# Requesting the first tiles of p_v from expert tile 118 on instead of 112, in a two-layer decoder trunk

## The chip, the cores and the metric

The kernel runs on one core of one Trainium2 chip. The metric is the device time of one execution in microseconds (us); the time of a kernel is the median of its runs. The profile is one execution, recorded by the hardware profiler; its times count from the start of its span.

## The reference

The program is a decoder trunk of two layers over 256 positions of width 1024. Each layer is an attention mixer (latent attention in layer 0, native sparse attention in layer 1) followed by a PEER feed-forward block, with a LayerNorm after each. Only the PEER block matters here. It holds 128 x 128 = 16,384 experts. Each position picks 16 experts for each of 8 heads by product keys, and the result is a sum over the picked experts:

```python
def peer_ffn(x, w_q, subkeys, u, v):
    ...
        experts = jnp.take_along_axis(cand_idx, pos, axis=-1)
        g = jax.nn.softmax(best, axis=-1)
        u_e = u[experts]
        v_e = v[experts]
        a = jax.nn.gelu(jnp.einsum("thkd,td->thk", u_e, xc, ...), approximate=False)
        return jnp.einsum("thk,thkd->td", (g * a).astype(v.dtype), v_e)
```

`u` and `v` are 16,384 x 1024 float32 each, 64 MB per layer and matrix.

## The kernel before

**Tiles.** All weights pass through one list, the stream, in the order in which they are used. For a PEER block the stream holds 128 tiles of `p_u` and then 128 tiles of `p_v`. A tile has 128 partitions x 1024 float32, which is 512 KB. The kernel does not gather experts for most positions: it multiplies every expert tile with 160 of the 256 positions (`xF`), and a matrix `A` holds the gate of each expert and position, zero where the expert was not picked. For the other 96 positions (partly for `u`, partly for `v`) it gathers single expert rows with indirect DMAs: 96 rows of 128 partitions x 4 KB from `p_ur`, then 64 from `p_v`.

**The u loop** (line 918) has one step per tile of `p_u`. `u_step(j)` runs 8 matmuls against `xF` (16 records in the profile, since each float32 matmul leaves two), straight from the tile that the DMA wrote. After every second step ScalarE applies gelu (`u_act`, L882) and VectorE multiplies it into `A` (L891). Between the steps VectorE also makes the one-hot matrices (`hot`, L759 to L770) that give the gates, and multiplies the gathered rows (`row`, L578).

**The v loop** uses the tiles of `p_v` in order. ScalarE rounds each to `hi` (L179), VectorE makes the remainder `lo` (L193), and TensorE multiplies both with parts of `A` (`W`, L900 and L905) into `acc`. In it VectorE adds the gathered rows of `p_v` (L600, L602).

**Who requests what.** All tiles are requested on SyncE's DMA queue (SP), which issues in the order of the program and waits, request by request, for the buffer to be free. Tiles of `p_u` are requested by `_snat` (line 149). From tile 96 on only five buffers serve them: tile j+5 is requested when TensorE has finished step j. Tiles of `p_v` are requested by `_sdma` (lines 120 and 125), two at a time as one request of 1024 KB where their place in the ring allows it. The pairs are (0,1), (2,3), (4,5), (6,7) in layer 0; in layer 1 tile 0 goes alone and then (1,2), (3,4), (5,6). They go to two rings of four tiles, `raw` and `spare`. The rows are requested by GpSimd (line 565) on a queue of its own, and a ring of six rows limits them.

**How far ahead of use p_v is requested.** `_ahead()` gives the last stream index that may be requested, and `self.vlim` caps it. At the start of a PEER block `vlim` is `v0 - 1`, where `v0` is the index of the first tile of `p_v`, so nothing of it is requested. At step `LATE` = 112 `gather()` sets up the second ring, `spare`. From that step on every even step raises `vlim` by 2:

```python
                u_step(j)
                if j == LATE:
                    self.gather()
                if j >= LATE and j % 2 == 0:
                    self.vlim += 2
```

`u_step` ends with `end()`, which first requests the next tile of `p_u`, then requests up to the limit that the step before had computed (`held`), and then computes a new one. A raise after step j is therefore seen at the end of step j+1 and put to use at the end of step j+2: the first tiles of `p_v` stand in SP's program behind the request that waits for step 114. After the loop `vlim` is lifted altogether. Independently of the limit, `nxt` of steps 125, 126 and 127 puts the `hi` copies of tiles 0, 1 and 2 of `p_v` into ScalarE's program, and those of 126 and 127 the `lo` of tiles 0 and 1 into VectorE's.

Of the kernel before, what the change touches and what calls it, by code (L numbers as in the profile page):

```python
# [42 lines left out]
SPREAD, LATE = 96, 112  # L43
# [4 lines left out]
class Kern:  # L48
# [471 lines left out]
    def peer(self, l):  # L520
# [3 lines left out]
        with ExitStack() as es:  # L524
# [44 lines left out]
            def g_x():  # L569
                for q in range(P // GX):  # L570
                    nc.gpsimd.dma_start(xrow[q * GX:q * GX + GX], self.hD[P - GT - GX:P - GT, 1, :])
                for hh in range(2):
                    nc.gpsimd.dma_start(gacc[hh * GT:hh * GT + GT], self.hD[P - GT:P, 1, :])

            def g_dot(k):
                a, c = order[k]
                t, x, d = grow.pop((a, c)), *((gacc, gdot) if a == "n" else (xrow, xdot))
                nc.vector.scalar_tensor_tensor(t, t, 1.0, x, op0=OP.mult, op1=OP.mult, accum_out=d[:, c:c + 1])  # L578
                if (a, c) == ("x", GX - 1):
                    g_row()  # L580
                    nc.scalar.activation(xdot, xdot, AF.Gelu)
                    self.defer(2, x_weights)
                g_row()
# [9 lines left out]
            def g_weights():  # L593
                nc.scalar.activation(gdot, gdot, AF.Gelu)
                nc.vector.tensor_tensor(ggate, ggate, gdot, op=OP.mult)
# [152 lines left out]
            def g_gen(hot):  # L748

                b4 = [P, 2, P, 2]  # L750
                for t0 in range(0, ND, 4):
                    while len(gq) == 2:
                        yield None
                    h = hot[:, t0 // 4 % 2]
                    if t0 >= NU:
                        h = h.bitcast(BF16)
                    oi, oj = h[:, 0], h[:, 1]
                    tt = nc.vector.tensor_tensor
                    tt(h[:, 0:2].rearrange("p w g i s -> p (w g) i s"), self.iota4[:, 0, None].to_broadcast([P, 4, P, 2]),  # L759
                       selI[:, t0 // 4].rearrange("p w (g s) -> p (w g) s", s=2)[:, :, None, :].to_broadcast([P, 4, P, 2]),  # L760
                       op=OP.is_equal); yield 0.64
                    if t0 < NU:
                        b5 = [P, 2, 2, P, 2]
                        tt(h[:, 2:4], oj[:, None].to_broadcast(b5),
                           selG[:, t0 // 4].rearrange("p w (g s) -> p w g s", s=2)[:, :, :, None, :].to_broadcast(b5), op=OP.mult)
                        gq.append((t0, oi, (h[:, 2], h[:, 3])))
                    else:
                        for o, i in ((h[:, 2], 0), (h[:, 3], 1), (oj, 2)):
                            x = selX[:, i, t0 - NU:t0 - NU + 4].rearrange("p (g s) -> p g s", s=2)
                            tt(o, oj, x[:, :, None, :].to_broadcast(b4), op=OP.mult)  # L770
                        gq.append((t0, oi, (h[:, 2], h[:, 3], oj)))
                    yield 0.64
# [4 lines left out]
            def g_flush(n=1):  # L777
                if len(gq) < n:
                    return
                while gq:  # L780
                    t0, oi, gs = gq.popleft()
                    ps = self.acc(t0 // 4 % 2)
                    for q in range(4):
                        for w, g in enumerate(gs):
                            self.mm(ps[:, q * P:(q + 1) * P], oi[:, q // 2, :, q % 2], g[:, q // 2, :, q % 2],
                                    w == 0, w == len(gs) - 1)
                    pv = ps.rearrange("p (t j) -> p j t", t=4)
                    k, sc_ = (done["a"], 1.0 / GS) if t0 < NU else (0, 1.0)
                    for x, j0, n in A:
                        m = min(max(k, 0), n)  # L790
                        if m > 0:
                            y = x[:, 0:m, t0:t0 + 4]
                            nc.vector.scalar_tensor_tensor(y, pv[:, j0:j0 + m], 1.0 / GS, y, op0=OP.mult, op1=OP.mult)  # L793
                        if m < n:
                            nc.scalar.activation(x[:, m:n, t0:t0 + 4], pv[:, j0 + m:j0 + n], AF.Copy, scale=sc_)  # L795
                        k -= n
                    done["g"] = t0 + 4
# [3 lines left out]
            def run_side(budget):  # L801
                credit[0] = min(credit[0] + budget, 2 * budget)
                paused = False
                while credit[0] > 0 and (first and not paused or second):
                    side = first if first and not paused else second
                    try:
                        cost = next(side[0])
                        if cost is None:
                            if paused or side is second:
                                return  # L810
                            paused = True
                        else:
                            credit[0] -= cost
                    except StopIteration:
                        side.popleft()
# [51 lines left out]
            def u_step(j):  # L867
                w, _ = self.nxt()
                if j % 2 == 0:
                    bank[j] = self.ps().rearrange("p (a t) -> p a t", a=2)  # L870
                ps = bank[j - j % 2][:, j % 2, 0:NU]
                for k in range(KC):
                    self.mm(ps, w[:, k * P:(k + 1) * P], xf[0][:, k, :], k == 0, k == KC - 1)
                self.end()
# [3 lines left out]
            def u_act(j):  # L878
                ps, n = bank.pop(j), min(done["g"], NU)
                y = slots((P - FIRST + j) % P, 2)  # L880
                if n:
                    nc.scalar.activation(ps[:, :, 0:n], ps[:, :, 0:n], AF.Gelu)  # L882
                    due.append((y[:, :, 0:n], ps[:, :, 0:n]))
                if n < NU:
                    nc.scalar.activation(y[:, :, n:NU], ps[:, :, n:NU], AF.Gelu)  # L885
                done["a"] = j + 2

            def u_mul():
                while due:
                    y, ps = due.pop()  # L890
                    nc.vector.tensor_tensor(y, y, ps, op=OP.mult)  # L891
# [16 lines left out]
            def w_start():  # L908
                W.append(self.pr8.tile([P, 5, 3 * P], F32R, tag="r8", name="W"))
                for j in range(3):  # L910
                    w_hi(j)
                w_lo(0)
                w_lo(1)
# [4 lines left out]
            for j in range(P):  # L918
                if j == 5:
                    g_x()  # L920
                g_flush(2)
                u_step(j)
                if j == LATE:
                    self.gather()
                if j >= LATE and j % 2 == 0:
                    self.vlim += 2
                self.slow = j < P - 7
                if j % 2:
                    u_mul()
                elif j:  # L930
                    u_act(j - 2)
                run_side(GB if len(A) > 1 else 2.1 if dj is None or j < dj else 1.15)
                if dj is None and gnext[0]:
                    dj = j + 2
                if not (first or second) and len(A) == 1:
                    es_r.close()

                    hot = self.pr8.tile([P, 2, 4, 2, P, 2], F16, tag="r8", name="hot")
                    A.append((pool(es_1, "slots1").tile([P, P - FIRST, ND], F32, name="A1"), 0, P - FIRST))
                    second.append(g_gen(hot))  # L940
                while dj and dc < len(order) and j >= dj + int((P - 6 - dj) / len(order) * dc):
                    g_dot(dc)
                    dc += 1
                    if dc == len(order):
                        g_weights()
                if done["g"] == ND and j >= P - 5 and not W:
                    w_start()
# [860 lines left out]
```

## Time and profile before

| | us |
|---|---|
| median of 3 runs | 1617.3 |
| lowest and highest run | 1615.9 and 1619.71 |
| the profiled execution | 1614.72 |
| its span in the profile | 1612.9 |

The profile lists, for each engine, its busy time and its instructions. PE is TensorE, DVE VectorE, ACT ScalarE, POOL GpSimd and SP SyncE. A row of the timeline gives start, duration, engine, line, operation and operands (written<-read), and in brackets how long the engine had been idle before and what it had waited for. PEclk is the share of its full clock that TensorE was granted. A row of the DMA view gives operands, queue, count, size and the median time from request to landing. The PEER block's u loop ends at 485.4 us in layer 0 and at 1311.9 us in layer 1.

### The profile page before, as it was taken

How to read it: one execution, taken by the hardware profiler on the slowest of the kernel's cores; microseconds unless marked ns; L12 is line 12 of the kernel's file. 1: busy time of each engine (PE TensorE's matmuls, PEld its weight loads, DVE VectorE, ACT ScalarE, POOL GpSimd, SP SyncE). 2: the span in 40 equal slices, each digit the busy share in tenths (PEclk: the TensorE clock that was granted, in tenths of full speed). 3: DMA queues.
4: the chain of work that ended last, by engine and by line, in shares of the span. 5: the costliest groups of instructions: out<-in, count | busy, mean ns of one | idle time of the engine just before them, and what ended most of it. 6: DMA issues, size and time to landing. Idle time of an engine off the chain costs nothing.

```text
span 1612.9 us, 27544 instructions
## 1 busy us (share of the span) xinstructions
PE 1559.4 (97%) x10018; PEld 1399.2 (87%) x10018; DVE 1396.6 (87%) x3245; ACT 683.1 (42%) x1355; POOL 517.6 (32%) x442
## 2 busy tenths in 40 slices
PE   7999999999989999999997999999999989999997
PEld 6779999999988888888885789999999978888886
DVE  5778798999949999999768789799999859999998
ACT  6555201222125555556466754111121245555553
POOL 2010134433325444331432210344343324443420
PEclk9999999999999999999999999999999999999999
DMA  7527999999998999998573258999999979999992
GB/s 241 196 89 232 351 409 408 409 408 345 394 375 319 368 371 343 356 355 296 188 259 96 67 183 282 400 408 409 408 398 354 385 307 390 355 361 343 364 352 92
DMA packets 140519, 510.76 MB, mean 317 GB/s; under 512 B 14144, under 2 KB 17248, under 8 KB 139296
## 3 DMA queue, kind: packets, MB, share of 16 engines
q1 hardware_dynamic: 90416, 325.75, 54.6%
q0 software_dynamic: 49968, 183.26, 30.0%
q8 instruction: 79, 1.29, 0.3%
q14 instruction: 56, 0.46, 0.1%
HBM read 503.19 MB, written 5.24 MB: 315 GB/s over the span
## 4 chain that ended last, share of the span: by engine, by line
PE 77%; DVE 11%; DMA 8%; ACT 2%; issue 1%; POOL 0%; SPq 0%; ACTq 0%; DVEq 0%; POOLq 0%
PE acc L273 44%; PE mm L273 31%; DMA row<-p_ur,xidx 5%; DVE row L578 3%; DMA nat<-p_u 3%; PE mm L300 1%; DVE hot L759 1%; DVE hot L770 1%; DMA xT<-xT 0%; DMA bounce<-ropeO 0%; DVE idx L641 0%; DVE lo L193 0%; DVE bnst L347 0%; ACT hi L179 0%; ACT p L1689 0%
## 5 line engine op out<-in xcount | busy, mean ns | idle before, releaser
L273 PE MATMUL acc<-hi,W 128*128 128x512 f32 x1452 | 409.1, 390 | 0.0
L273 PE MATMUL mm<-xF,nat 128*128 128x160 f32 x2304 | 328.7, 303 | 10.6 <-DMA nat<-p_u 10.5
L565 POOL DMA_INDIRECT row<-p_v,gidx x128 | 228.2, 1783 | 336.7 <-DVE gacc L602 257.7
L273 PEld LDWEIGHTS mm<-xF,nat 128*128 128x128 f32 x2304 | 320.0, 193 | 12.1 <-issue 11.4
L273 PEld LDWEIGHTS acc<-hi,W 128*128 128x128 f32 x1452 | 272.5, 188 | 57.5
L273 PE MATMUL acc<-lo,W 128*128 128x512 f32 x968 | 298.8, 390 | 0.0
L193 DVE TENSOR_TENSOR lo<-raw,hi 128x1024 fp32r<-128x1024 f32 (+1 forms) x203 | 246.8, 1223 | 33.9 <-ACT hi L179 28.6
L179 ACT CAST hi<-raw 128x1024 fp32r<-128x1024 f32 (+1 forms) x207 | 215.0, 1045 | 142.4 <-PE acc L273 116.5
L565 POOL DMA_INDIRECT row<-p_ur,gidx x128 | 138.7, 1084 | 280.0 <-DVE row L578 190.3
L273 PEld LDWEIGHTS acc<-lo,W 128*128 128x128 f32 x968 | 181.8, 188 | 38.4
L179 ACT CAST hi<-spare 128x1024 fp32r<-128x1024 f32 x122 | 128.2, 1051 | 111.2 <-PE acc L273 109.2
L602 DVE SCALAR_TENSOR_TENSOR gacc<-row,ggate,gacc 128x1024 f32<-128x1024 f32 x126 | 160.9, 1277 | 0.0
L193 DVE TENSOR_TENSOR lo<-spare,hi 128x1024 fp32r<-128x1024 f32 x122 | 148.7, 1219 | 11.9 <-ACT hi L179 11.9
L578 DVE SCALAR_TENSOR_TENSOR row<-row,gacc 128x1024 f32<-128x1024 f32 x128 | 155.4, 1217 | 0.0
L273 PE MATMUL mm<-xF,more 128*128 128x160 f32 x896 | 125.7, 300 | 0.0
L273 PE MATMUL mm<-xF,raw 128*128 128x160 f32 x896 | 125.5, 300 | 0.0
L273 PEld LDWEIGHTS mm<-xF,more 128*128 128x128 f32 x896 | 122.6, 190 | 0.0
L273 PEld LDWEIGHTS mm<-xF,raw 128*128 128x128 f32 x896 | 122.5, 190 | 0.0
L795 ACT ACTIVATE A<-acc 128x208 f32<-128x208 f32 (+19 forms) x116 | 37.5, 346 | 194.3 <-DVE A L793 167.6
L885 ACT ACTIVATE A<-mm 128x320 f32<-128x320 f32 (+13 forms) x104 | 38.1, 368 | 172.7 <-PE mm L273 171.0
L905 DVE TENSOR_TENSOR W<-A,W 128x128 fp32r<-128x128 f32 (+1 forms) x512 | 107.0, 250 | 0.0
L565 POOL DMA_INDIRECT row<-p_ur,xidx x64 | 65.7, 1027 | 95.9 <-DVE row L578 43.5
(289 smaller groups left out, 2071.1 us busy)
## 6 DMA issues: line engine op xcount, KB each, us to landing
nat<-p_u SPq DMA_DIRECT2D x144, 512.0 KB, 9.2
spare<-p_v SPq DMA_DIRECT2D x64, 1024.0 KB, 8.8
raw<-p_v SPq DMA_DIRECT2D x63, 1024.0 KB, 8.8
raw<-p_u SPq DMA_DIRECT2D x56, 512.0 KB, 14.8
more<-p_u SPq DMA_DIRECT2D x56, 512.0 KB, 15.9
raw<-p_wq SPq DMA_DIRECT2D x32, 512.0 KB, 4.2
raw<-b_wo SPq DMA_DIRECT2D x12, 512.0 KB, 3.7
raw<-a_wo SPq DMA_DIRECT2D x8, 512.0 KB, 3.7
```

Source lines behind the costliest of these rows:

```text
L179: self.nc.scalar.copy(self.his[i], self.raws[i])
L193: e.tensor_tensor(self.los[i], raw, self.his[i].bitcast(F32), op=OP.subtract)
L273: self.nc.tensor.matmul(out, a, b, start=start, stop=stop)
L300: self.nc.tensor.transpose(out, in_, self.ident[:n, :n])
L565: nc.gpsimd.indirect_dma_start(out=t, out_offset=None, in_=table, in_offset=bass.IndirectOffsetOnAxis(ap=at, axis=0))
L578: nc.vector.scalar_tensor_tensor(t, t, 1.0, x, op0=OP.mult, op1=OP.mult, accum_out=d[:, c:c + 1])
L602: nc.vector.scalar_tensor_tensor(gacc, t, ggate[:, c:c + 1], gacc, op0=OP.mult, op1=OP.add)
L759: tt(h[:, 0:2].rearrange("p w g i s -> p (w g) i s"), self.iota4[:, 0, None].to_broadcast([P, 4, P, 2]), selI[:, t0 // 4].rearrange("p w ( ...
L770: tt(o, oj, x[:, :, None, :].to_broadcast(b4), op=OP.mult)
L795: nc.scalar.activation(x[:, m:n, t0:t0 + 4], pv[:, j0 + m:j0 + n], AF.Copy, scale=sc_)
L885: nc.scalar.activation(y[:, :, n:NU], ps[:, :, n:NU], AF.Gelu)
L905: nc.vector.tensor_tensor(WW[j][:, o:o + c.stop - c.start], slot(j)[:, c], WW[j][:, c].bitcast(F32), op=OP.subtract)
```

## The change

The first raise of the limit moves by six steps, from step 112 to step 118. Five even steps are left in the loop (118, 120, 122, 124, 126) where there were eight. The second ring is still set up at step 112.

```diff
                 if j == LATE:
                     self.gather()
-                if j >= LATE and j % 2 == 0:
+                if j >= LATE + 6 and j % 2 == 0:
                     self.vlim += 2
```

In SP's program the requests of the first eight tiles of `p_v` (seven in layer 1) then stand at the ends of steps 120, 122 and 124 and, for the last of them, in step 126, instead of at the ends of steps 114, 116, 118 and 120. The request of the last tile of `p_u`, tile 127, stands at the end of step 122 in both kernels. The change applies to the PEER blocks of both layers.

## The prediction

> **What bounds the kernel now.** I read the page first, then the chain of work that ended last, then the timeline around the places where the chain leaves TensorE. From the page:
>
> ```profile
> span 1612.9 us, 27544 instructions
> PE 1559.4 (97%) x10018; PEld 1399.2 (87%) x10018; DVE 1396.6 (87%) x3245; ACT 683.1 (42%) x1355; POOL 517.6 (32%) x442
> L273 PE MATMUL mm<-xF,nat 128*128 128x160 f32 x2304 | 328.7, 303 | 10.6 <-DMA nat<-p_u 10.5
> ```
>
> TensorE is busy 97% of the span, so only its gaps and its slow stretches can be won. The third row has one: 10.5 us of waiting for tiles of p_u, over both layers. TensorE's timeline shows where: at the end of the u loop, in layer 0
>
> ```profile
> 452.72 11.56 PE L273 MATMUL mm<-xF,nat 128*128 128x160 f32 x80
> 469.45 15.97 PE L273 MATMUL mm<-xF,nat 128*128 128x160 f32 x96 [5.17 <-DMA nat<-p_u]
> ```
>
> and in layer 1:
>
> ```profile
> 1278.78 11.63 PE L273 MATMUL mm<-xF,nat 128*128 128x160 f32 x80
> 1295.57 11.58 PE L273 MATMUL mm<-xF,nat 128*128 128x160 f32 x64 [5.16 <-DMA nat<-p_u]
> ```
>
> A step has 16 records, and the 96 records from 469.45 are the loop's last six steps, so TensorE ends step 121 at 452.72 + 11.56 = 464.28 and then waits 5.17 us for tile 122. Layer 1 stops at the same step, at 1290.41. The chain says what steps cost undisturbed, and when the v loop follows in each layer:
>
> ```profile
> 436.98 6.57 PE mm L273 x48
> ```
>
> ```profile
> 485.42 288.02 PE acc L273 x1266
> ...
> 1311.92 291.18 PE acc L273 x1280
> ```
>
> 48 records are three steps, so a step is 6.57 / 3 = 2.19 us. Six steps should take 13.14 us, but those from 469.45 took 15.97. The busy times by stage say why (PEclk is the first of the last three numbers):
>
> ```profile
> 464.28:469.45 5.17, 0.00 (x1) 0.03 (x1) 1.16 (x5) 1.18 (x4) 0.00 (x0) 0.87 1.02 408
> 469.45:474.95 5.50, 5.50 (x21) 5.50 (x22) 0.00 (x0) 0.00 (x0) 0.00 (x0) 0.50 1.02 409
> 474.95:485.42 10.47, 10.47 (x78) 10.47 (x78) 3.34 (x4) 3.69 (x5) 0.00 (x0) 1.00 0.73 282
> ```
>
> After the gap the granted clock is 0.50 for 5.50 us, and full again. So the stop costs more than its own length: from 464.28 to the v loop at 485.42 are 21.14 us, 8.00 more than six steps need. In layer 1, 1311.92 - 1290.41 = 21.51 us, 8.37 more.
>
> What is tile 122 waiting behind? SP's timeline for layer 0 (nat is p_u; raw and spare are p_v's pairs 0/1, 2/3, 4/5 and 6/7):
>
> ```profile
> 447.86 0.38 SPq L120 DMA_DIRECT2D raw<-p_v  x1
> 449.36 2.50 SPq L149 DMA_DIRECT2D nat<-p_u  x2
> 451.91 0.43 SPq L120 DMA_DIRECT2D raw<-p_v  x1
> 455.14 2.50 SPq L149 DMA_DIRECT2D nat<-p_u  x2
> 457.69 0.56 SPq L120 DMA_DIRECT2D spare<-p_v  x1
> 459.49 2.67 SPq L149 DMA_DIRECT2D nat<-p_u  x2
> 462.20 0.43 SPq L120 DMA_DIRECT2D spare<-p_v  x1
> 464.31 10.10 SPq L149 DMA_DIRECT2D nat<-p_u  x2
> ```
>
> The last number of these rows of the DMA view is the time to landing, of tile 122,
>
> ```profile
> nat<-p_u SPq DMA_DIRECT2D x1, 512.0 KB, 14.2
> ```
>
> of v4/5 and tile 123,
>
> ```profile
> spare<-p_v SPq DMA_DIRECT2D x1, 1024.0 KB, 16.4
> nat<-p_u SPq DMA_DIRECT2D x1, 512.0 KB, 14.3
> ```
>
> and of v6/7 and tile 125:
>
> ```profile
> spare<-p_v SPq DMA_DIRECT2D x1, 1024.0 KB, 17.0
> nat<-p_u SPq DMA_DIRECT2D x1, 512.0 KB, 14.9
> ```
>
> Tile 122 is requested at 455.14, when step 117 frees its buffer, and lands 14.2 us later, at 469.3: just before TensorE goes on. It is 9.14 us from its request to the point where it is wanted (464.28). Just before the first request of p_v a tile of p_u took 4.9 us (request at 443.7):
>
> ```profile
> nat<-p_u SPq DMA_DIRECT2D x1, 512.0 KB, 4.9
> ```
>
> Between the two, SP put 2 x 1024 KB of p_v ahead of tile 122, and GpSimd six rows of p_v on its own queue, which share the same bandwidth:
>
> ```profile
> L565 POOL DMA_INDIRECT row<-p_v,gidx x6: 943/945/1688, 449.7 to 459.5; - x6
> 455.00:470.00 15.00, 9.79 (x67) 9.19 (x67) 4.56 (x12) 2.18 (x7) 3.79 (x4) 0.94 1.03 410
> ```
>
> At 410 GB/s the DMA is full (its share is 1.03). 512 KB (0.524 MB) take 1.28 us alone.
>
> **The change, part by part.** No instruction is added or removed; four requests per layer move in SP's program. What decides is the order of bytes in SP's queue, and the requests land in that order in every row above. Summed up from tile 119's request, in KB, layer 0 before: u119 512, v0/1 1536, u120 2048, u121 2560, v2/3 3584, u122 4096 (lands 469.3), u123 4608 (457.31 + 14.3 = 471.6), v4/5 5632 (457.69 + 16.4 = 474.1), u124 6144, u125 6656 (461.83 + 14.9 = 476.7), v6/7 7680 (462.20 + 17.0 = 479.2).
>
> After, u119 to u125 come first (3584), then v0/1 4608, u126 5120, u127 5632, and v2/3 6656, v4/5 7680, v6/7 8704. Behind u127 no request for p_u holds SP back, so v2/3 to v6/7 go out right behind it, at about 467. If the full DMA moves the same bytes by the same time, v0/1 lands at 471.6, u126 midway to 474.1, at 472.85, u127 at 474.1, v2/3 at 476.7, v4/5 at 479.2 and v6/7 2.56 us later, at 481.8.
>
> Against that the wants, without a stop: step 122 begins at 464.28, 126 at 464.28 + 4 x 2.19 = 473.04, 127 at 475.23, the v loop at 477.42. Tiles 122 to 125 stand at 2048 to 3584 KB, which before had landed ahead of 469.3 - 2.5 = 466.8 at the latest; step 125 begins at 470.85. So the stop at 122 goes. **Next late is u126**, behind v0/1: it has 0.19 us to spare.
>
> For layer 1 the same, with the requests of v1/2, of u122 (with u123) and of v3/4, and their times to landing in that order:
>
> ```profile
> 1277.97 0.53 SPq L120 DMA_DIRECT2D raw<-p_v  x1
> 1281.20 2.50 SPq L149 DMA_DIRECT2D nat<-p_u  x2
> 1283.74 0.44 SPq L120 DMA_DIRECT2D spare<-p_v  x1
> ```
>
> ```profile
> raw<-p_v SPq DMA_DIRECT2D x1, 1024.0 KB, 14.9
> ```
>
> ```profile
> nat<-p_u SPq DMA_DIRECT2D x1, 512.0 KB, 14.2
> ```
>
> ```profile
> spare<-p_v SPq DMA_DIRECT2D x1, 1024.0 KB, 17.1
> ```
>
> They land at 1292.9, 1295.4 and 1300.8, where 3072, 3584 and 5120 KB are through. After: u125 3584 (1295.4, wanted 1296.98), v0 4096, u126 4608 (two thirds of the way: 1299.0, wanted 1299.17), u127 5120 (1300.8, wanted 1301.36), v1/2 6144 (1303.4). The v loop would begin at 1303.55 and want tile 1 at 1305.8.
>
> "The same bytes by the same time" fails where the DMA was not full before and p_v used that room:
>
> ```profile
> 1273.00:1280.00 7.00, 7.00 (x67) 6.96 (x66) 6.93 (x14) 1.74 (x5) 2.67 (x4) 1.00 0.95 335
> ```
>
> Here 335 GB/s moved, so v0 went partly into free room; moved behind, it costs later requests between 0 and its own 1.28 us. In layer 0 v0/1 costs 0 to 2.56. I take half a tile, 0.6 us, in both, since the room between 335 and 410 GB/s is about as large as v0 itself. u126 is then late by 0.6 - 0.19 = 0.4 us in layer 0 and 0.6 - 0.17, also 0.4, in layer 1; u127 gains 0.9 us per tile on a step and isn't late.
>
> What else hangs on p_v's first tiles is the split (ACT, then DVE, layer 0 before):
>
> ```profile
> 476.76 0.42 ACT L882 ACTIVATE mm<-mm 128x320 f32<-128x320 f32 x1 [11.27 <-PE mm L273]
> 477.10 1.98 ACT L179 CAST hi<-raw 128x1024 fp32r<-128x1024 f32 x2
> ```
>
> ```profile
> 478.17 2.36 DVE L193 TENSOR_TENSOR lo<-raw,hi 128x1024 fp32r<-128x1024 f32 x2 [0.46 <-ACT hi L179]
> ```
>
> hi and lo of a tile are 1 and 1.2 us. From 471.6 both tiles of v0/1 are split by 475.5, under 2 us ahead of the v loop, on two engines that idle there (ACT for 11.27 us before). Behind the waiting copy on ACT stands only the gelu of steps 124/125, which TensorE doesn't need in the loop's last steps. v2/3 is wanted two v steps of 288.02 / 128 = 2.25 us after 477.42, at 481.9, v4/5 at 486.4; with 2.3 us of splitting each is in time by 2.9 us or more. Cost: none. If that cover goes, it is the rival below.
>
> For gaps of 0.4 us I count no halving of the clock; the rows show one after 5.17 us only. The Trainium skill, TensorE: Matmul & The Clock Gate, What's actually happening, has the clock drop after an idle window of about 3.4 us. This trace agrees (5.17 us, then 0.50). By that page a gap of 0.4 us costs its length alone and the sum stands; were the clock halved for it too, 2 x 2.83 us (15.97 - 13.14) would go, 1607.5, inside the range.
>
> Sum: 8.00 + 8.37 - 0.4 - 0.4, about 15.5 us. The profiled execution of 1614.72 becomes 1599.2, and the median, which lies 2.6 us above it, 1617.3 - 15.5 = **1601.8 us**.
>
> **The rivals.** (a) *The stop moves to u126.* If the queue serves v0/1 and u126 at half the rate beside the rows, v0/1 takes 5.1 us instead of 2.56: u126 lands at 466.8 + 5.1 + 2.6 = 474.5, 1.4 us late, and u127 2.6 later, 0.3 late again. 1.7 us per layer leave a gain of 13.0, 1604.3. At 3 us of idle with a halved clock (2.83 us, 15.97 - 13.14), 5.8 us are lost per layer, and 4.7 gained in all: 1612.6. For it: the thin margin. Against: the last row is requested at 459.5, and the more of the DMA the rows get early, the sooner SP's queue has it alone.
>
> (b) *The rows alone are enough.* At half of 410 GB/s tiles of p_u come at 205, and the loop wants 512 KB per 2.19 us, 239. If their backlog outgrows the lead of 8.76 us (four steps), tile 122 is late without any p_v: 1617. Against: 34 GB/s short over the 15 us of the rows is 0.5 MB, 2.5 us at 205, on top of 4.9. The Trainium skill, DMA: Bandwidth & Descriptors, Queues, rings and completion order, has each engine go round robin between its queues, which is this case; by it the rows get their half whatever SP asks for. The landings agree: v1/2 at 1292.9, u122 at 1295.4, 2.5 us for 512 KB. The same price holds if the later limit does not order the requests as I read it.
>
> (c) *The v loop starves (slower).* Place: its first eight tiles, which today lie ready when it starts. If SP's queue stays at half the rate beyond 1295.4, the pairs land at 1308.2, 1313.3 and 1318.4, 5.1 us apart, while the loop uses a pair in 4.5. Stalls: 1.7 in steps 126 and 127, 3.0 at v tile 1, 0.6 each at tiles 3 and 5, 2.8 for one halved clock, and 0.6 for each of eight more pairs: 13.5 against 8.2 won, so 5.3 slower per layer, 1627.9. It decides from a delay of 8 us at the start of the v loop on. Against: GpSimd has no row left to ask for until the v loop frees one.
>
> **How the numbers follow.** Forecast 0.72, (a) 0.14, (b) 0.08, (c) 0.06. Forecast and (a) are faster, (b) is the same, (c) slower; 0.2%, 3.2 us, is about what a measurement here can tell. Low end: all 16.37 us, less the 1.4 us by which the fastest run lies below the median, 1599.5. High end: 1610, most of (a); above it lie its rest, (b) and (c).
>
> **What would show it.** Right: SP's first request of p_v at about 462 and 1288, behind tile 125; tiles 122 to 125 landing in under 8.7 us; no halved clock at the loop's end; the v loop at about 477.8 and 1304; 10.5 us of waiting for p_u down to 1 or so. Wrong: an idle gap of over 3 us at steps 126 or 127, PEclk of 0.50 there, or a wait of TensorE for hi or lo in the first ten v tiles.

## The result and the profile after

The changed kernel takes 1604.82 us (median of 6 runs, 1602.16 to 1606.3) against 1617.72 for the kernel before in the same comparison (6 runs, 1613.3 to 1619.75). The ratio is 0.9921, with a 95% interval of 0.9908 to 0.9934: 12.9 us faster, where the prediction had 15.5 less and 1601.8. Its profiled execution took 1603.88 us. From its page and its groups of instructions:

```profile
span 1601.9 us, 27548 instructions
PE 1557.4 (97%) x10018; PEld 1396.3 (87%) x10018; DVE 1396.6 (87%) x3245; ACT 683.6 (43%) x1355; POOL 536.3 (33%) x442
L273 PE MATMUL mm<-xF,nat 128*128 128x160 f32 x2304 | 323.0, 300 | 1.9 <-DMA nat<-p_u 1.9
```

The wait of TensorE for tiles of p_u is down from 10.5 us to 1.9. The span is 11.0 us shorter. SP's timeline at the end of layer 0's u loop shows the new order:

```profile
461.99 0.43 SPq L120 DMA_DIRECT2D raw<-p_v  x1
463.78 2.50 SPq L149 DMA_DIRECT2D nat<-p_u  x2
466.33 0.43 SPq L120 DMA_DIRECT2D raw<-p_v  x1
466.81 1.01 SPq L120 DMA_DIRECT2D spare<-p_v  x2
```

The pair v0/1 goes out at 461.99, behind u125. Then come u126 and u127, and right behind them, with nothing to hold SP back, the other three pairs. TensorE's timeline, layer 0 first, then layer 1:

```profile
452.67 15.68 PE L273 MATMUL mm<-xF,nat 128*128 128x160 f32 x112
468.56 4.92 PE L273 MATMUL mm<-xF,nat 128*128 128x160 f32 x32 [0.21 <-DMA nat<-p_u]
474.95 4.58 PE L273 MATMUL mm<-xF,nat 128*128 128x160 f32 x32 [1.48 <-DMA nat<-p_u]
479.27 0.73 PE L273 MATMUL acc<-hi,W 128*128 128x512 f32 x2
```

```profile
1276.33 19.87 PE L273 MATMUL mm<-xF,nat 128*128 128x160 f32 x144
1296.36 4.58 PE L273 MATMUL mm<-xF,nat 128*128 128x160 f32 x32 [0.16 <-DMA nat<-p_u]
1300.68 0.73 PE L273 MATMUL acc<-hi,W 128*128 128x512 f32 x2
```

The gap of 5.2 us at step 122 is gone in both layers. What is left waits for tile 126 (and 0.21 us for tile 124). A measure into which time lost ahead of it does not enter is the time from the start of step 117 (452.67 and 1276.33 here, 452.72 and 1278.78 before) to the first matmul of the v loop (485.15 and 1311.65 in the timeline of before). I use it below for every kernel, as "the last eleven steps". Each row has one profile; the two profiles of the same kernel differ by up to 1.2 us in it.

| kernel | last eleven steps, layer 0 | layer 1 | median, us | ratio to before (interval) |
|---|---|---|---|---|
| before: limit raised from step 112 | 32.43 | 32.87 | 1616.7 to 1617.7 | 1 |
| the change: from step 118 | 26.60 | 24.35 | 1604.82 | 0.9921 (0.9908 to 0.9934) |
| the change, again | 25.39 | 24.55 | 1602.17 | 0.9909 (0.9894 to 0.9924) |
| from step 116 | 29.27 | 28.07 | 1608.67 | 0.9943 (0.9925 to 0.9960) |
| from step 120 | 24.78 | 24.90 | 1601.44 | 0.9897 (0.9878 to 0.9916) |
| from step 120, again | 23.85 | 24.19 | 1602.87 | 0.9914 (0.9900 to 0.9929) |
| before, rows of p_v held back | 25.94 | 25.24 | 1603.31 | 0.9908 (0.9886 to 0.9929) |
| from step 120, rows held back | 23.85 | 23.86 | 1601.81 | 0.9908 (0.9891 to 0.9925) |
| before, extra matmuls | 34.45 | 31.60 | 1618.41 | 1.0003 (0.9989 to 1.0017) |
| from step 124, SP gated | 30.33 | 31.73 | 1620.81 | 1.0026 (1.0014 to 1.0038) |
| four tiles early, rest from step 120 | 24.11 | 23.86 | 1613.83 | 0.9990 (0.9977 to 1.0003) |

By this measure the change won 5.83 + 8.52 = 14.35 us, 1.2 less than the 15.57 of the prediction's sum. The span shows only 11.0 of it. Most of the rest went between the layers. These are the stretches of layer 0's end in the stages of the changed kernel (the third number from the end is PEclk)

```profile
775.90:779.30 3.40, 1.60 (x8) 1.24 (x9) 3.02 (x6) 0.59 (x1) 3.40 (x7) 1.00 0.51 189
779.30:786.10 6.80, 6.13 (x18) 4.48 (x17) 4.90 (x5) 1.63 (x2) 0.05 (x1) 0.50 0.96 340
```

and the same work in the kernel before:

```profile
781.80:785.20 3.40, 1.58 (x8) 1.22 (x9) 3.03 (x6) 0.58 (x1) 3.40 (x7) 1.00 0.50 178
785.20:792.00 6.80, 6.12 (x30) 4.84 (x29) 5.23 (x5) 1.64 (x2) 0.03 (x1) 1.00 0.97 366
```

TensorE is busy 1.6 us of 3.4 in both, in short pieces. Then the clock is halved for 6.8 us in one profile and not in the other. By the chain, the v loop ended 5.92 us earlier than before (767.96 against 773.88), but the first large product after it began only 3.06 us earlier (789.75 against 792.81): 2.86 us lost. The last section shows why one profile has it and the other not.

### The profile page after: what moved, and what is told of

Read it like the earlier page. It is cut to its first block, busy times and chain, and to the rows that moved or that the text cites. A ratio compares the mean times of both kernels' runs of the same rounds, so it can differ in the third digit from the quotient of the medians.

```text
span 1601.9 us, 27548 instructions
## 1 busy us (share of the span) xinstructions
PE 1557.4 (97%) x10018; PEld 1396.3 (87%) x10018; DVE 1396.6 (87%) x3245; ACT 683.6 (43%) x1355; POOL 536.3 (33%) x442
## 4 chain that ended last, share of the span: by engine, by line
PE 78%; DVE 10%; DMA 8%; ACT 2%; issue 1%; POOL 0%; SPq 0%; ACTq 0%; DVEq 0%; POOLq 0%
PE acc L273 45%; PE mm L273 32%; DMA row<-p_ur,xidx 6%; DVE row L578 3%; PE mm L300 1%; DMA nat<-p_u 1%; DMA raw<-a_wv 1%; DVE hot L759 1%; DVE hot L770 1%; DMA xT<-xT 1%; DVE lo L193 0%; DVE idx L641 0%; DVE bnst L347 0%; ACT hi L179 0%; ACT p L1689 0%
## 5 line engine op out<-in xcount | busy, mean ns | idle before, releaser
L565 POOL DMA_INDIRECT row<-p_v,gidx x128 | 245.1, 1915 | 305.3 <-DVE gacc L602 238.1
L273 PE MATMUL mm<-xF,nat 128*128 128x160 f32 x2304 | 323.0, 300 | 1.9 <-DMA nat<-p_u 1.9
L273 PEld LDWEIGHTS mm<-xF,nat 128*128 128x128 f32 x2304 | 314.6, 190 | 3.1 <-issue 2.5
L193 DVE TENSOR_TENSOR lo<-spare,hi 128x1024 fp32r<-128x1024 f32 x122 | 148.8, 1219 | 10.5 <-ACT hi L179 10.5
```

What stands on the lines that cost most here:

```text
L193: e.tensor_tensor(self.los[i], raw, self.his[i].bitcast(F32), op=OP.subtract)
L273: self.nc.tensor.matmul(out, a, b, start=start, stop=stop)
L565: nc.gpsimd.indirect_dma_start(out=t, out_offset=None, in_=table, in_offset=bass.IndirectOffsetOnAxis(ap=at, axis=0))
```

## The experiments

The theory: what makes tile 122 late is the number of bytes ahead of it while the DMA is full, in SP's own queue and in the rows that GpSimd asks for. The rivals: the rows alone or SP's order alone do it, any shift behind tile 122 is as good, or a v loop whose first tiles come late gives the gain back. All edits below are against the kernel before.

**The limit from step 120 on.**

```diff
-                if j >= LATE and j % 2 == 0:
+                if j >= LATE + 8 and j % 2 == 0:
```

> The limit is raised from step 120 on (8 later than before), so that all requests of p_v stand behind the last one of p_u. My theory (the order of bytes in SP's queue decides when a tile of p_u lands): in layer 0 the stall of 1.5 us at step 126 and most of the 0.7 us around steps 124 and 125 go, v0/1 lands 2.6 us later, at about 476, and its split still ends near the start of the v loop; the v loop starts 1 to 2 us earlier than with the change (478 instead of 479.5), in layer 1 0 to 0.2 us earlier; in all about 1603 to 1604, 13.5 to 15 us under before, unless the clock is halved in other places. Rival (the v loop starves when p_v comes last): TensorE waits for hi or lo in the first v tiles, 2 us or more per layer, and the time is 1607 or more.

Measured: 1601.44 us, ratio 0.9897 (0.9878 to 0.9916). All of p_v now stands behind u127. In layer 0:

```profile
452.23 15.90 PE L273 MATMUL mm<-xF,nat 128*128 128x160 f32 x112
468.34 8.94 PE L273 MATMUL mm<-xF,nat 128*128 128x160 f32 x64 [0.21 <-DMA nat<-p_u]
477.01 0.73 PE L273 MATMUL acc<-hi,W 128*128 128x512 f32 x2
477.95 0.73 PE L273 MATMUL acc<-lo,W 128*128 128x512 f32 x2 [0.20 <-DVE lo L193]
```

The stop at step 126 is gone, and the last eleven steps take 24.78 us instead of 26.60; in layer 1, 24.90 instead of 24.35, no gain. The last row shows the other end of the scale: TensorE waits 0.20 us for the lo of the first tile. ScalarE's first hi starts at 475.60, 1.4 us ahead of the v loop. The v loop doesn't starve, but no room is left. The time was below what I expected (1603 to 1604); a repeat further down gave 1602.87, so part of that was chance.

**The limit from step 116 on.**

```diff
-                if j >= LATE and j % 2 == 0:
+                if j >= LATE + 4 and j % 2 == 0:
```

> The limit is raised from step 116 on, between before (112) and the change (118): v0/1 stands ahead of u124, v2/3 ahead of u126. My theory: tiles 122 and 123 are in time, and tile 124 is late by about the time that v0/1 takes beside the rows: step 124 stalls 3.6 us in layer 0, and 2.0 us in layer 1, where v0 is half as large. The clock is halved in layer 0 at most. Time between the two: 1608 to 1613. Rival (any shift behind tile 122 is enough, the stall was one of tile 122 only): as with the change, 1605.

Measured: 1608.67 us, 0.9943 (0.9925 to 0.9960), as the theory had it. The stop sits where the first p_v stands in the queue, at tile 124, and is about as long as expected in both layers:

```profile
472.36 10.61 PE L273 MATMUL mm<-xF,nat 128*128 128x160 f32 x64 [3.51 <-DMA nat<-p_u]
...
1294.46 10.61 PE L273 MATMUL mm<-xF,nat 128*128 128x160 f32 x64 [2.30 <-DMA nat<-p_u]
```

The rival (any shift behind tile 122 is enough) is out. One expectation failed: the clock is halved after both stops, also after the one of 2.30 us (stages of the same kernel, layer 1; PEclk 0.62 in the second):

```profile
1292.16:1294.46 2.30, 0.00 (x1) 0.03 (x1) 1.35 (x2) 1.37 (x2) 0.00 (x0) 1.00 1.03 411
1294.46:1298.90 4.44, 4.43 (x20) 4.44 (x21) 0.37 (x1) 0.06 (x1) 0.00 (x0) 0.62 1.03 411
```

**The rows held back, SP's order as before.** GpSimd's first six rows of p_v are not issued in the loop of the dot products; a small copy that reads the products of step 122 holds GpSimd until they are there, and the rows follow (at 469.95 us and after, instead of 449.66). This is the second part of the edit; the first lets `g_row` count the rows of p_v instead of requesting them:

```diff
+                if j == P - 3:
+                    t = self.small.tile([P, 1], F32, tag="aside", name="aside")
+                    nc.gpsimd.tensor_copy(t, slot((P - FIRST + j - 3) % P)[:, 0:1])
+                    hold[0] = False
+                    for c in range(owed[0]):
+                        g_row()
```

> The kernel before (limit from step 112 on), but the first six gathered rows of p_v are requested only once step 123 is done, some 20 us later. My theory (both queues share one full DMA): with the rows out of the way the DMA has room for p_v ahead of tile 122, so the stall at step 122 goes here as well, with no change of SP's order; the v loop starts at about 477.5, the time is near 1603, plus up to 3 us if the first row comes late for the v loop's VectorE. Rival (the order in SP's own queue alone makes tile 122 late, whatever GpSimd asks for): the stall of 5 us and the halved clock stay, 1617.

Measured: 1603.31 us, 0.9908 (0.9886 to 0.9929). With the limit still raised at step 112, the stop of 5 us is gone:

```profile
463.98 4.59 PE L273 MATMUL mm<-xF,nat 128*128 128x160 f32 x32 [0.36 <-DMA nat<-p_u]
469.09 4.58 PE L273 MATMUL mm<-xF,nat 128*128 128x160 f32 x32 [0.53 <-DMA nat<-p_u]
474.16 4.58 PE L273 MATMUL mm<-xF,nat 128*128 128x160 f32 x32 [0.49 <-issue]
```

In layer 1 a stop of 1.14 us is left, at tile 126. So neither queue makes tile 122 late by itself. The early p_v and the rows together are too much for the DMA in these 25 us, and taking either away is enough to end the stop of 5 us.

**Extra matmuls in the gap.** The kernel before computes 18 more products ahead of step 122, whose result nothing uses.

```diff
+                if j == 122:
+                    fill = self.ps()
+                    for k in range(18):
+                        self.mm(fill[:, 0:NU], self.ident, xf[0][:, 0, :], k == 0, k == 17)
```

> The kernel before, with 18 extra matmuls of the same shape (xF against the identity, result unused) ahead of step 122, which take about 4.9 us and keep TensorE busy while tile 122 is on its way. My theory (the lost clock is a price of the idle time, 2.8 us per layer): tile 122 lands as before, the extra matmuls cost nothing, the granted clock stays 1.00 and the v loop starts at 482.6 instead of 485.4 in layer 0, 2.8 to 3.2 us earlier in layer 1 too: about 1612. Rival (the halved clock has another cause, or the extra matmuls are simply added): 1617 to 1627.

Measured: 1618.41 us, 1.0003 (0.9989 to 1.0017); the expected 6 us did not come. In layer 0 the profile doesn't answer the question, since here tile 120 was late already (2.10 us) and the clock was halved ahead of the extra work. The program up to there is that of the kernel before, so that much varies from one execution to the next. Layer 1 does. Its timeline, and the stages with PEclk:

```profile
1296.69 5.05 PE L273 MATMUL mm<-xF,ident 128*128 128x160 f32 x36
1301.58 4.60 PE L273 MATMUL mm<-xF,nat 128*128 128x160 f32 x32
1307.94 4.58 PE L273 MATMUL mm<-xF,nat 128*128 128x160 f32 x32 [1.76 <-DMA nat<-p_u]
1313.06 4.58 PE L273 MATMUL mm<-xF,nat 128*128 128x160 f32 x32 [0.54 <-DMA nat<-p_u]
```

```profile
1296.69:1301.58 4.89, 4.89 (x39) 4.89 (x37) 1.16 (x5) 1.18 (x4) 0.00 (x0) 1.00 1.03 408
1301.58:1316.00 14.42, 12.13 (x88) 11.63 (x87) 3.43 (x4) 3.69 (x5) 0.00 (x0) 1.00 0.93 373
```

The extra work filled the gap and the clock stayed at 1.00. Yet TensorE, now at full speed, ran into tiles 124 and 126 and waited 1.76 and 0.54 us there. The last eleven steps took 31.60 us instead of 32.87. In the kernel before, TensorE at half speed had used up time in which the DMA wasn't ready anyway: tile 126 landed 16.8 us after its request at 1290.44, at 1307.2, and step 126 started at 1307.33. So the queue set the end of the u loop there, and the halved clock cost about 1.3 us, not the 2.83 that I had taken as a price of its own. This rests on one layer of one profile of each kernel.

**SP gated behind the last tile.** The limit is raised from step 124 on, and SP first writes 128 x 4 bytes to memory and reads them back.

```diff
+                if j == LATE + 12:
+                    gate = self.dram.tile([P, 1], F32, tag=f"gate{l}", name=f"gate{l}")
+                    t = self.small.tile([P, 1], F32, tag="aside", name="aside")
+                    nc.sync.dma_start(gate, self.lneps)
+                    nc.sync.dma_start(t, gate)
-                if j >= LATE and j % 2 == 0:
+                if j >= LATE + 12 and j % 2 == 0:
```

> All of p_v behind the last request of p_u, and SP first sends a 128 x 4 byte write and reads it back, so that it asks for p_v only once tile 127 has landed (about 474.5 in layer 0). My theory: v0/1 then lands at about 479.5, its hi is ready 1 us later, and TensorE, done with the u loop at about 477, waits 3 to 4 us in each layer for the first tile; with a halved clock after the wait 1 to 3 us more per layer: 1609 to 1615, the gain mostly given back. It prices the cover of the split: about 2 us of room behind the order with no such gate. Rival (the start of the v loop has room for a later p_v, since the rings refill): within 2 us of the kernel that raises the limit from step 120, 1601 to 1604.

Measured: 1620.81 us, 1.0026 (1.0014 to 1.0038), worse than expected. SP's timeline in layer 0:

```profile
468.07 0.44 SPq L928 DMA_DIRECT2D gate<-lneps  x1
478.15 0.33 SPq L929 DMA_DIRECT2D aside<-gate  x1
478.52 0.95 SPq L120 DMA_DIRECT2D raw<-p_v  x2
```

The write of 512 bytes alone took 10 us, behind tiles of p_u that were still under way; SP held the read back until it had landed and asked for p_v right after issuing the read. So p_v was requested 4 us later than I had assumed. The first matmuls of the two v loops:

```profile
484.73 1.22 PE L273 MATMUL acc<-hi,W 128*128 128x512 f32 x2 [4.74 <-ACT hi L179]
...
1313.54 1.22 PE L273 MATMUL acc<-hi,W 128*128 128x512 f32 x2 [7.61 <-ACT hi L179]
```

So a v loop that starves can take the whole gain, as the prediction's third rival had it, but at another place (the first tile, not tile 1 and those behind it) and with the first pair requested at 478.5 instead of 466 in layer 0, which is 10.3 us later counted from the start of step 117; no delay in between was tried. The clock was halved after both waits: these pairs of matmuls took 1.22 us where the other kernels need 0.73. Behind these two waits TensorE doesn't wait for a hi again in either v loop: it is the first request of p_v that matters, the others catch up.

**Four tiles early.** By step 96 p_u has left the ring `raw`, so that half of the tiles can come 14 steps ahead of the limit in the kernel before.

```diff
-                if j >= LATE and j % 2 == 0:
+                if j in (96, 98) or j >= LATE + 8 and j % 2 == 0:
```

> The first four tiles of p_v (three in layer 1) are requested from step 98 on, into the ring that p_u's tiles have left by then, the others behind the last request of p_u. My theory (what counts is the sum of bytes ahead of a tile of p_u while the DMA is full; between 410 and 447 us it moved 345 to 390 GB/s, not 410): some 2 MB fit into that room at the price of a later landing of the tiles of p_u around step 105, which have lead to spare; no stall at steps 105 or 122 to 127, hi and lo of the first tiles are ready early; 1600 to 1604, the same as the kernel that raises the limit from step 120 within 2 us. Rival (any p_v ahead of p_u in SP's queue costs TensorE its own transfer time, wherever it stands): a stall of 1.3 to 2.6 us per layer near step 105 and a halved clock after it, 1606 to 1612.

Measured: 1613.83 us, 0.9990 (0.9977 to 1.0003). My theory's number failed, and the rival's size was nearer. The end of the u loop is clean (24.11 and 23.86 us), but stops are back earlier, at steps 104 and 106 of layer 0 (the first two rows) and at step 106 of layer 1, each just behind a request of p_v of 1024 KB:

```profile
422.19 6.26 PE L273 MATMUL mm<-xF,nat 128*128 128x160 f32 x32 [2.54 <-DMA nat<-p_u]
432.27 8.44 PE L273 MATMUL mm<-xF,nat 128*128 128x160 f32 x48 [2.90 <-DMA nat<-p_u]
...
1254.24 4.91 PE L273 MATMUL mm<-xF,nat 128*128 128x160 f32 x32 [2.77 <-DMA nat<-p_u]
```

I had read rates of 345 to 390 GB/s as room. They were none: from 410 to 447 us the share was 1.01, at 389 GB/s. Around the two requests (at 407.25 and 412.57) the kernel before, first row, moved 403 GB/s at a DMA share of 1.02, this one 384 at 1.01:

```profile
405.00:420.00 15.00, 15.00 (x131) 14.93 (x130) 14.93 (x33) 2.74 (x10) 5.52 (x6) 1.00 1.02 403
...
405.00:420.00 15.00, 14.65 (x126) 14.33 (x124) 14.93 (x33) 2.76 (x11) 6.41 (x6) 1.00 1.01 384
```

The DMA engines are as busy; they move less in the same time. Here the share, not GB/s, told that there was no room.

**The change and the limit from step 120 again, side by side, and both measures together.**

> The changed kernel a second time, beside the next two on the same chip. It had one halved clock of 6.8 us between layer 0 and layer 1 that the kernel before and the one with the limit from step 120 did not show, at a place where the code is the same. If that is a matter of where the clock's windows happen to fall, the profile need not show it again (span 1599 instead of 1601.9), while stalls of about 1.5 us at step 126 and 0.7 around step 124 in layer 0 come back; if the changed order causes it, it is there again. Median 1602 to 1606.

> The limit from step 120 on a second time. If the order behind the last tile of p_u is what makes it better than the change, the v loop of layer 0 starts some 2 us earlier than in the changed kernel again, and the median is 1 to 3 us lower; if the 3.4 us between the two medians were chance, they are equal within 1 us.

> Both: the limit from step 120 on and the first six rows of p_v requested once step 123 is done. My theory: with the DMA to themselves the last tiles of p_u land in 5 to 7 us, so the small waits of 0.2 to 0.6 us at steps 123 to 125 go as well; that is all that is left at this place: 0 to 1.5 us per layer, less what a late first row costs VectorE in the v loop. 1599 to 1602. Rival (the u loop's end is still bound by the DMA with the limit at step 120): 3 us or more.

Measured on one chip: the change 1602.17 us, 0.9909 (0.9894 to 0.9924); the limit from step 120, 1602.87, 0.9914 (0.9900 to 0.9929); that with the rows held back, 1601.81, 0.9908 (0.9891 to 0.9925). The three are the same, and the lead of 3.4 us that the limit from step 120 had over the change in the first two measurements did not come back. In the last eleven steps they differ as before: 25.39 us in layer 0 with the change, whose stop at step 126 came back with 1.30 us, and 23.85 in both others, which is eleven steps without a wait (11 x 2.19 = 24.1; the v loop's first matmul overlaps the last of them). What offsets this in the profiles is the place between the layers. The changed kernel, which had the halved clock there in its first profile, doesn't have it in this one; both others have it. By the chain, the 26 matmuls at that place took 6.23 us in the changed kernel now,

```profile
779.83 6.23 PE acc L273 x26
```

8.54 in its first profile and 8.04 in the limit from step 120 now. Of the eleven profiles, four have this stretch halved: one of the change's two, one of the two with the limit from step 120, the one with both measures and the one with the extra matmuls, which requests p_v as the kernel before does. Its code is the same in all of them. The order of requests alone does not decide it; what does is in the last section.

## Why the prediction was right, and where it was off

**The mechanism** stood: the stop at step 122 came from the bytes ahead of tile 122, and it goes when p_v's first pairs go behind. In the changed kernel tile 122 lands 8.2 us after its request instead of 14.2:

```profile
nat<-p_u SPq DMA_DIRECT2D x1, 512.0 KB, 8.2
```

The rival that the rows alone would be enough is refuted by this row, since the rows go out as before; and the rows held back show the other half, that p_v ahead of tile 122 isn't enough alone either.

**The next to be late** was tile 126, as forecast, with 1.48 and 0.16 us instead of 0.4 and 0.4. In layer 0 that is the size that rival (a) named (1.4 us), and its 1604.3 lies nearer to the median of 1604.82 than the forecast does. Its mechanism was not seen: v0/1 landed 2.6 us behind u125, at the full rate and not at half of it (the rows below). One sign that the prediction asked for failed: tiles 124 and 125 took 9.0 and 9.4 us to land, not under 8.7, and tile 124 was 0.21 us late.

**The mis-sized term** in layer 0 is "the same bytes by the same time", with half a tile taken off for room that p_v had used. Tile 125 was to land by 466.8. These are the times to landing of v0/1 and u125 in the changed kernel, and then of u126:

```profile
raw<-p_v SPq DMA_DIRECT2D x1, 1024.0 KB, 11.6
nat<-p_u SPq DMA_DIRECT2D x1, 512.0 KB, 9.4
```

```profile
nat<-p_u SPq DMA_DIRECT2D x1, 512.0 KB, 11.0
```

u125 landed at 461.6 + 9.4 = 471.0, and u126 at 463.8 + 11.0 = 474.8, 2.0 us behind the 472.85 of the plain sum, where I had allowed 0.6. The stage behind it, in the kernel before (first row) and in the changed one:

```profile
449.00:455.00 6.00, 6.00 (x60) 5.96 (x59) 5.37 (x12) 1.74 (x5) 3.36 (x3) 1.00 1.01 404
...
449.00:455.00 6.00, 6.00 (x60) 5.96 (x59) 5.32 (x12) 1.74 (x5) 3.41 (x3) 1.00 0.98 342
```

342 GB/s moved where the kernel before had moved 404, at almost the same share. Over 449 to 465 us it was 371 against 408, which is 0.59 MB less, or 1.4 of the 2.0 us at 410 GB/s. In layer 1, where half as much stands ahead of tile 126, the sum was 0.5 us too small (8.52 against 8.37 - 0.4). So the two layers' errors partly cancel, and the total came nearer than its parts.

**The halved clock** was counted with 2.83 us per layer as if it could be won by itself. The sum is right, since it was made from the step ends, but the extra matmuls show for layer 1 that the queue, not the clock, set the end of the loop: tiles 124 and 126 would have been late at full speed too.

**Clock and gaps.** I counted no halving for gaps of 0.4 us, and none came for gaps of up to 1.76 us in the u loops' ends. But gaps of 2.10 us (the extra matmuls, layer 0) and 2.30 us (limit from step 116) were followed by 3.4 us of halved clock. The Trainium skill, TensorE: Matmul & The Clock Gate, What's actually happening, asks for an idle window of about 3.4 us; here less was enough, and the measurement decides. Nor does the length of the gap alone decide: the one of 2.77 us (four tiles early, layer 1) was followed by none.

**The total.** 15.57 us were forecast for the two stages; two profiles have 14.35 and 25.39 + 24.55 against 32.43 + 32.87, that is 15.36. The medians have 12.9 and 15.3. The first of the two profiles has the halved stretch between the layers (2.9 us), which the prediction took as unchanged, and the second has not; whether that also makes the difference between the two medians is not shown.

## What to carry to other kernels

A prefetch that stands ahead of a nearer request in the same queue costs that request its transfer time as soon as the DMA is full, so place it behind the last request that is due before it, and then check how much room its own first use has: here the limit from step 118 and from 120 on are equal, from 116 on costs 4 to 7 us, and a first request of p_v 10 us later gives the whole gain back. Look for room in the DMA by its busy share before you go by GB/s: here 389 GB/s at a share of 1.01 was no room. When a stall is followed by a slowed engine, ask whether the next input would have been there for a fast one before the slowdown gets a price of its own.

## What the runs showed of the hardware

The trace's clock records put the halved stretches on a fixed grid: in the kernel before they start at 468.1, 867.5, 888.0 and 1294.1 us, multiples of 3.413 us apart (117, 6 and 119 of them), and last 3.4 or 6.8 us. Whether a broken stretch is halved depends on how this grid cuts it. With the grid taken from each profile's own clock records, the eleven profiles have, from 15 to 1600 us, 37 windows of 3.41 us at full clock in which TensorE was busy 1.65 us or less: each was followed by a halved one. Of the 44 with 1.66 to 1.91 us 11 were, and of all those with more only one (2.33 us). Between the layers the last window ahead of the halved stretch has 1.57 us in the changed kernel (775.86 to 779.27); in the kernel before, the emptiest window there has 1.94 (782.15 to 785.56), and nothing follows. The gap of 2.30 us fell into one window and left it 1.11; the one of 2.77 us was cut by a grid line, and its two windows kept 2.34 and 1.71. Between the layers this is about 2.9 us won or lost by a kernel that changed nothing there. Halved clock also goes with much of the spread between runs: of the sixteen runs of the kernel before beside the first four experiments, the fastest took 1613.94 us at a mean granted clock of 0.992, the slowest 1622.92 at 0.987, and 0.005 of 1617 us are 8.1 of those 9.0 us. That is an estimate, since the clock is given to 0.001, which is 1.6 us, and part of the halved time stands behind stops of the queue. Why the DMA engines, at a busy share of 0.98 to 1.03, move 342 to 384 GB/s in some stretches and 403 to 410 in others is left open.
